# A seventh Strassen block in each channel mixer, and the DRAM weight sums issued during the token mixers

## The chip, the cores and the metric

The kernel runs on one core of one Trainium2 chip, as one launch. The metric is the device time of that launch in microseconds, the median over runs of the same kernel. The profile is of one further execution, taken with the hardware profiler.

## The reference

A two-layer encoder trunk on 512 tokens of width 1024, all in float32. Layer 0 mixes tokens by retention and neighbourhood attention, layer 1 by a bidirectional state-space scan. Each layer then has a channel mixer, and this is what the change is about:

```python
def conv_geglu_ffn(hn, w_up, conv_w, conv_b, w_down):
    u = depthwise_conv_centered(hn @ w_up, conv_w, conv_b)
    gate, val = jnp.split(u, 2, axis=-1)
    return (jax.nn.gelu(gate, approximate=True) * val) @ w_down
```

`hn` is 512 x 1024, `w_up` 1024 x 5632 (2816 gate columns and 2816 value columns), the convolution has width 3 along the tokens, `w_down` is 2816 x 1024. RMS norms stand before and after each mixer, and the result is added to the residual stream.

## The kernel before, in words

**Precision.** Every large product is made of three TensorE passes (`mm3`, L121 to L126): both operands are split into a high part in fp32r and the remainder, and high x high, high x low and low x high are accumulated. ScalarE makes the high part (L115, a cast), VectorE the low part (L116, a subtraction). Each weight tile of 128 x 1024 is split so into one of four places of a ring (`weight`, L81); a place comes free when TensorE has finished with the product four tiles earlier.

**The up projection** (`ffn`). The 2816 hidden columns are 22 tiles of 128, each with a gate and a value half. A plain tile takes two weight tiles of 128 x 1024 and 2 x 8 x 3 matmuls of 512 columns. Pairs of tiles can instead go through one Strassen-Winograd block (`up_strassen`), which forms the 2 x 2 block product of (gate, value) pair weights and (token half, channel half) inputs from seven products in place of eight. Each of the seven is 24 matmuls of 256 columns, 168 in a block. `UP` (L395) lists the first tiles of the blocks: 6, 8, 10 and 14, 16, 18, so two runs of three blocks with the plain tiles 12 and 13 between them; tiles 0 to 5, 20 and 21 are plain too. The combinations of the inputs are made once (`combos`) during tiles 2 to 5.

The seven products of a block (called first to seventh here) need these weight tiles, each split by ScalarE and VectorE: the first q11; the second q12, to which VectorE has added q22 (L458); the third the sum q0 = q11 + q12, made by VectorE; the fourth q0 + q21, added in place by VectorE; the fifth q11 again, to which a DMA issued by GpSimd has by then added another block of `w_up` (L473, an accumulating DMA into SBUF; it overwrites q11, so it waits until the first product's split and VectorE's sum q0 have read it); the sixth q21; the seventh q22. VectorE also does three additions of products (512 columns) in a block, and the tails: per tile four convolution steps (L519, L520) and one multiplication (L527). The tails of a block's two tiles are held back and called during the next block, after its fourth and sixth product, or at once when no block follows.

**The down projection** (`down_strassen`) uses Strassen too. Its combined weights are formed in DRAM: `sums` (L273) makes a list of 32 GpSimd DMAs of 704 KB for each layer ("sums" below), first 16 plain copies of quarters of `w_down`, then 16 accumulating ones. `E.chore()` (L68) issues the next of them and makes it wait for the latest matmul of `E.product`, which only `mm3` sets. Before the change they are issued from: the first pass of the output projection of layer 0's mixer (4), `c` in the last list of `SLOTS` in layer 1's mixer (4), the plain tiles, and `up_strassen` after the second, fourth and sixth product. One preparatory step of the down projection, a subtraction over half of the hidden activations (L320, 128 x 2816 elements, VectorE), needs only tiles 0 to 10.

**What sets the order.** A scheduler orders each engine's instructions when the program is built, by its own estimates; weight splits and loads run ahead of their products. Each engine then works through its list in order and waits where an operand is missing. Weight loads are issued by SyncE (L77, L450) into three `wst` buffers, two `gain` buffers and two `wu` buffers. `PAIRS` and `SLOTS` list the steps of the token mixers in the order in which they are written.

## Time and profile before

| what | value |
|---|---|
| median of 3 runs (lowest, highest) | 1366.14 us (1362.77, 1366.8) |
| the profiled execution | 1365.16 us, of which the span on the core is 1363.4 us |
| TensorE, VectorE, ScalarE, GpSimd busy | 98%, 81%, 61%, 9% of the span |
| DMA, mean over the span | 173 GB/s |
| layer 0: first run of three blocks | 340.88 to 398.47 us |
| layer 0: tiles 12 and 13 | 398.47 to 420.25 us |
| layer 0: second run of three blocks | 420.25 to 482.08 us |
| layer 1: the same three | 1088.34, 1145.93, 1167.72 to 1229.80 us |

The starts are those of the first matmul of each part. A matmul's row ends later than the next one starts, since matmuls are pipelined; what a part costs on TensorE is therefore the distance from its first start to the next part's first start. In the rows, `L126 PE` and so on name the line of the kernel and the engine, `out<-in` the tiles written and read, and `<-DVE ring L116` after an idle time the instruction that ended the wait. PE is TensorE, DVE VectorE, ACT ScalarE, POOL GpSimd, SP SyncE.

### The profile page before, as it was taken

The page shows a single profiled execution, that of the slowest core. Times are in us where ns is not written, and L with a number is a line of the kernel's source. Part 1 is how long each engine was busy: PE and PEld are TensorE (multiplying, and loading weights), DVE is VectorE, ACT ScalarE, POOL GpSimd, SP SyncE. Part 2 cuts the span into 40 slices and gives each one's busy share as a digit, 9 for nine tenths or more (in the row PEclk, how much of TensorE's full clock was granted, in tenths as well). Part 3 has the DMA queues.
Part 4 walks back from the last instruction along what each step waited for, and adds up shares of the span by engine and source line. Part 5 has one row for each costly group of instructions (what it writes and reads, how often), then busy time and mean ns, then how long its engine had stood idle before and what let it go on. Part 6 is the DMA issues. An engine that isn't in the chain of part 4 may idle for free.

```text
span 1363.4 us, 20143 instructions
## 1 busy us (share of the span) xinstructions
PE 1329.6 (98%) x7640; PEld 1135.2 (83%) x7640; DVE 1108.5 (81%) x1536; ACT 831.9 (61%) x1337; POOL 127.6 (9%) x142
## 2 busy tenths in 40 slices
PE   7999999999999999999999999999999999999997
PEld 6877777898998987888778788787879899898886
DVE  7368878696898889797878876898789789899876
ACT  5356667453674666564878787477555466466663
POOL 1011110100111100020000110011011011110001
PEclk9999999999999999999999999999999999999999
DMA  8443234246698966564565455175545678897654
GB/s 299 141 143 102 87 101 156 72 154 206 221 224 189 234 195 203 183 208 129 142 186 190 120 183 171 52 200 151 182 131 193 191 226 211 190 235 197 202 183 147
DMA packets 78785, 236.23 MB, mean 173 GB/s; under 512 B 8544, under 2 KB 9312, under 8 KB 78176
## 3 DMA queue, kind: packets, MB, share of 16 engines
q1 hardware_dynamic: 60368, 167.30, 38.1%
q0 software_dynamic: 10432, 52.43, 16.6%
q10 hardware_dynamic: 7888, 15.21, 4.0%
q8 instruction: 60, 0.98, 0.3%
q14 instruction: 37, 0.30, 0.1%
HBM read 227.30 MB, written 51.64 MB: 205 GB/s over the span
## 4 chain that ended last, share of the span: by engine, by line
PE 74%; DVE 10%; DMA 8%; ACT 4%; issue 3%; POOL 0%; SPq 0%; DVEq 0%; POOLq 0%; ACTq 0%
PE mm L124 20%; PE mm L126 20%; PE mm L125 19%; DMA wst<-in_f_up 3%; DVE ring L116 2%; PE pu L125 2%; DMA pb<-pd 2%; PE pu L126 2%; PE pu L124 2%; PE pi L1133 1%; PE st L1082 1%; ACT ring L115 1%; PE py L1153 1%; DMA wst<-in_c_fm 1%; ACT pb L1112 1%
## 5 line engine op out<-in xcount | busy, mean ns | idle before, releaser
L124 PE MATMUL mm<-xh,ring 128*128 128x512 f32 (+2 forms) x928 | 341.4, 368 | 1.4 <-ACT z L1052 1.0
L126 PE MATMUL mm<-xl,ring 128*128 128x512 f32 (+2 forms) x928 | 340.6, 368 | 1.1 <-DVE mean L936 0.6
L125 PE MATMUL mm<-xh,ring 128*128 128x512 f32 (+2 forms) x928 | 340.2, 367 | 1.0 <-DVE ring L116 1.0
L116 DVE TENSOR_TENSOR ring<-wst,ring 128x1024 fp32r<-128x1024 f32 (+1 forms) x220 | 267.2, 1221 | 61.5 <-ACT ring L115 61.3
L115 ACT CAST ring<-wst 128x1024 fp32r<-128x1024 f32 (+1 forms) x220 | 226.6, 1036 | 133.5 <-PE mm L125 54.0
L124 PEld LDWEIGHTS mm<-xh,ring 128*128 128x128 f32 (+1 forms) x928 | 174.4, 188 | 31.5 <-issue 2.3
L126 PEld LDWEIGHTS mm<-xl,ring 128*128 128x128 f32 (+1 forms) x928 | 174.0, 188 | 30.8 <-issue 1.3
L125 PEld LDWEIGHTS mm<-xh,ring 128*128 128x128 f32 (+1 forms) x928 | 174.4, 188 | 29.3 <-DVE ring L116 1.4
L1112 ACT ACTIVATE pb<-pb,tok 128x128 f32<-128x128 f32 x256 | 81.0, 397 | 10.4 <-DMA pb<-pd 9.3
L124 PE MATMUL mm<-xc,ring 128*128 128x256 f32 x288 | 79.9, 277 | 0.4 <-ACT G L500 0.4
L126 PE MATMUL mm<-xc,ring 128*128 128x256 f32 x288 | 79.8, 277 | 0.0
L125 PE MATMUL mm<-xc,ring 128*128 128x256 f32 x288 | 79.7, 277 | 0.0
L124 PE MATMUL mm<-ring,big 128*128 128x512 f32 x164 | 64.0, 390 | 0.0
L126 PE MATMUL mm<-ring,big 128*128 128x512 f32 x164 | 63.8, 389 | 0.0
L125 PE MATMUL mm<-ring,big 128*128 128x512 f32 x164 | 63.8, 389 | 0.0
L284 POOL DMA_DIRECT2D ts<-in_f_down x48 | 30.6, 638 | 308.2 <-PE mm L126 197.9
L125 PE MATMUL pu<-xh,ring 128*128 128x256 f32 x192 | 54.2, 282 | 4.2 <-DVE ring L116 4.2
L518 ACT ACTIVATE cv<-mm,cwt 128x512 f32<-128x512 f32 x40 | 31.0, 776 | 42.5 <-PE mm L126 42.5
L124 PEld LDWEIGHTS mm<-xc,ring 128*128 128x128 f32 x288 | 54.0, 188 | 0.6 <-ACT G L500 0.6
L126 PEld LDWEIGHTS mm<-xc,ring 128*128 128x128 f32 x288 | 54.1, 188 | 0.0
L125 PEld LDWEIGHTS mm<-xc,ring 128*128 128x128 f32 x288 | 54.0, 188 | 0.0
L126 PE MATMUL pu<-xl,ring 128*128 128x256 f32 x192 | 53.8, 280 | 0.0
(360 smaller groups left out, 3068.8 us busy)
## 6 DMA issues: line engine op xcount, KB each, us to landing
ts<-in_f_down POOLq DMA_DIRECT2D x48, 704.0 KB, 7.1
wst<-in_f_up SPq DMA_DIRECT2D x64, 512.0 KB
wst<-in_c_fm SPq DMA_DIRECT2D x40, 512.0 KB
wst<-ts SPq DMA_DIRECT2D x32, 512.0 KB
pb<-pd ACTq DMA_DIRECT2D x29, 512.0 KB
wst<-in_f_down SPq DMA_DIRECT2D x24, 512.0 KB
ts<-ts POOLq DMA_DIRECT2D x16, 704.0 KB, 9.2
wst<-in_ab_fm SPq DMA_DIRECT2D x20, 512.0 KB
```

What stands on the lines that cost most here:

```text
L115: first = self.nc.scalar.copy(hi, src)
L116: second = self.nc.vector.tensor_tensor(lo, src, hi.bitcast(F32), op=ALU.subtract)
L124: mm(out, lh, rh, start=first, stop=False)
L125: mm(out, ll, rh, start=False, stop=False)
L126: self.product = mm(out, lh, rl, start=False, stop=last)
L284: out.append(lambda i=i, src=src, j=j, c=c, kw=kw: gp.dma_start(part(ts, i, c), part(src, j, c), **kw))
L518: nc.scalar.activation(o, ps, AF.Identity, scale=w(1), bias=w(3))
L1082: nc.tensor.matmul(ps, o["bt"][:, c], xs, start=True, stop=True)
L1112: nc.scalar.activation(pb[:, dr, c], pb[:, dr, c], AF.Identity, scale=1.0 - 2 * dr, bias=tok[:, 0, c, dr * H + h:dr * H + h + 1])
L1133: nc.tensor.matmul(pi[:, c - 1 + dr], o["st"][dr, i][:, q * P:(q + 1) * P], o["t"][1][:, c * C:(c + 1) * C], start=True, stop=True)
L1153: E.together([nc.tensor.matmul(py[j * 64:j * 64 + 64, c * C:(c + 1) * C], o["x"][:, c, (2 * q + j) * 64:(2 * q + j + 1) * 64], ms[j][0][:, c],
```

## The change

Three edits. `UP` gets the entry 12, so tiles 6 to 19 are seven Strassen blocks in a row. `up_strassen` issues a sum after its second and fifth product (before: second, fourth, sixth); the held tails are called where they were. `PAIRS` and three lists of `SLOTS` get steps `c`, each of which issues one sum: 15 in layer 0's mixer, 8 more in layer 1's; and `ret_values` sets `E.product`, so that a sum after it waits for its matmuls.

```diff
-UP = (6, 8, 10, 14, 16, 18)
+UP = (6, 8, 10, 12, 14, 16, 18)
...
-        if i in (1, 3, 5):
+        if i in (1, 4):
             E.chore()
-            if i > 1 and held:
-                held.pop(0)()
+        if i in (3, 5) and held:
+            held.pop(0)()
...
 PAIRS = (
-    "nq rq rk nk rg k d s0 m a0 a1 v0 w0 s2 a2 a3 v2 w1 w2 n w3 o",
+    "nq rq rk nk rg c k d s0 m a0 a1 v0 c w0 s2 a2 a3 v2 c w1 w2 n w3 o",
...
             E.together(ms, [w for _, w in o["sd", i]])
+            E.product = ms[-1]
...
+                elif step == "c":
+                    E.chore()
...
 SLOTS = (
...
-    "s0 G R s1 s2 h0 i0 i1 o0 h1 h2 o1 p0 h4 h3 p1 h5 i2 n0 n1 p2 n6 n3 h6 n7 n2 n9 N i3 n8 h7 p3 n4 n5 N",
+    "s0 G R s1 s2 h0 i0 i1 o0 c h1 h2 o1 c p0 h4 h3 p1 h5 i2 n0 c n1 p2 n6 c n3 h6 n7 n2 n9 N i3 n8 h7 p3 n4 n5 N",
```

What it moves. On TensorE, ScalarE and VectorE the token mixers' instructions stand in the same order as before, and on SyncE too. TensorE loses, in each layer, the 96 matmuls of tiles 12 and 13 and gets one more block of 168.

VectorE, layer 0, where the second run of blocks began before (`gain_3988` is that block's q0, `wst_4167` its follower's q12; the second row is the sum that the fourth product needs, the last its split):

```order
L520 SCALAR_TENSOR_TENSOR cv0_3910<-mm_3856,cwt_2543,cv0_3910 128x511
L458 TENSOR_TENSOR gain_3988<-gain_3988,gain_4018 128x1024
L458 TENSOR_TENSOR wst_4167<-wst_4167,wu_4169 128x1024
L320 TENSOR_TENSOR H_2519<-H_2519 128x11x256
L519 SCALAR_TENSOR_TENSOR cv1_3915<-mm_3885,cwt_2543,cv1_3915 128x511
L116 TENSOR_TENSOR ring_69<-gain_3988,ring_69 128x1024
```

VectorE after the change, from the split for the fifth block's first product (`wst_4009`) to those for its second and third (`wst_4038`, `gain_4070`):

```order
L116 TENSOR_TENSOR ring_69<-wst_4009,ring_69 128x1024
L320 TENSOR_TENSOR H_2534<-H_2534 128x11x256
L458 TENSOR_TENSOR V_3776<-w5_3937,V_3776 128x2x256
L458 TENSOR_TENSOR G_3775<-pu_3779,G_3775 128x2x256
L519 SCALAR_TENSOR_TENSOR cv0_3967<-G_3544,cwt_2558,cv0_3967 128x511
L116 TENSOR_TENSOR ring_69<-wst_4038,ring_69 128x1024
L520 SCALAR_TENSOR_TENSOR cv0_3967<-G_3544,cwt_2558,cv0_3967 128x511
L519 SCALAR_TENSOR_TENSOR cv1_3972<-V_3545,cwt_2558,cv1_3972 128x511
L116 TENSOR_TENSOR ring_69<-gain_4070,ring_69 128x1024
```

The subtraction L320 has moved from just ahead of the split for a fourth product to just behind the split for a first.

ScalarE before, in the third block (`gain_3598` is q0, `wst_3536` is q11 after its accumulating DMA):

```order
L518 ACTIVATE cv1_3664<-V_3300,cwt_2543,cwn_2545 128x512
L115 CAST ring_69<-gain_3598 128x1024
L500 COPY G_3531<-mm_3533 128x2x256
L115 CAST ring_69<-wst_3536 128x1024
L525 ACTIVATE cv0_3659<-cv0_3659 128x512
```

ScalarE after the change, in the sixth block (`gain_4299` is q0, first as the third product's weights and then as the fourth's; `wst_4238` is q11 after its accumulating DMA; `gain_4329` is q21):

```order
L115 CAST ring_69<-gain_4299 128x1024
L500 COPY G_4233<-mm_4235 128x2x256
L115 CAST ring_69<-wst_4238 128x1024
L500 COPY V_4234<-pu_4236 128x2x256
L115 CAST ring_69<-gain_4299 128x1024
L115 CAST ring_69<-gain_4329 128x1024
```

In the first four blocks the cast for the fourth product stands ahead of the one for the fifth; in the fifth, sixth and seventh it stands behind it, in both layers, and so do the splits on VectorE:

```order
L458 TENSOR_TENSOR gain_4299<-wst_4238,wst_4267 128x1024
L519 SCALAR_TENSOR_TENSOR cv0_4359<-G_4004,cwt_2558,cv0_4359 128x511
L527 TENSOR_TENSOR H_2534<-cv0_4196,cv1_4201 128x512
L116 TENSOR_TENSOR ring_69<-gain_4299,ring_69 128x1024
L520 SCALAR_TENSOR_TENSOR cv0_4359<-G_4004,cwt_2558,cv0_4359 128x511
L458 TENSOR_TENSOR gain_4299<-gain_4299,gain_4329 128x1024
L116 TENSOR_TENSOR ring_69<-wst_4238,ring_69 128x1024
L519 SCALAR_TENSOR_TENSOR cv1_4364<-V_4005,cwn_2560,cv1_4364 128x511
L116 TENSOR_TENSOR ring_69<-gain_4299,ring_69 128x1024
```

These nine rows begin with the sixth block's sum q0, after which its accumulating DMA can start, and end with the split for its fourth product.

GpSimd in layer 0's mixer, before and after the change (`rb` is the rotary multiplication of a head pair, `rs` its group norm):

```order
L737 TENSOR_TENSOR rb_679<-rb_679,rot_234 128x512
L737 TENSOR_TENSOR rb_985<-rb_985,rot_234 128x512
L826 TENSOR_TENSOR rs_924<-rs_924,rg_760 128x512
L737 TENSOR_TENSOR rb_1032<-rb_1032,rot_234 128x512
L737 TENSOR_TENSOR rb_1373<-rb_1373,rot_234 128x512
```

```order
L737 TENSOR_TENSOR rb_679<-rb_679,rot_234 128x512
L284 DMA ts0_220<-in_f0_down 16x11264 x3
L737 TENSOR_TENSOR rb_988<-rb_988,rot_234 128x512
L827 TENSOR_TENSOR rs_927<-rs_927,rg_760 128x512
L737 TENSOR_TENSOR rb_1035<-rb_1035,rot_234 128x512
L284 DMA ts0_220<-in_f0_down 16x11264 x4
```

The first head pair's three sums stand ahead of the next pair's first rotary step, the second pair's four ahead of the third pair's, and so on. Of the 32 sums of layer 0, 13 are left to its channel mixer (28 before): 7 in the plain tiles and 2 in each of the first three blocks, none after that. In layer 1 it is 20 (28 before), the last of them in the seventh block.

8 rows, old and new, of tables (PAIRS, SLOTS) are left out of this document.

## The prediction

> **What bounds the kernel now.** I read the page's first lines, then who TensorE waits for, longest first in total (us in total, times, longest).
>
> ```profile
> span 1363.4 us, 20143 instructions
> PE 1329.6 (98%) x7640; PEld 1135.2 (83%) x7640; DVE 1108.5 (81%) x1536; ACT 831.9 (61%) x1337; POOL 127.6 (9%) x142
> PE pt L181 <- DVE xs L172: 10.2, 5, 7.3
> PE pu L125 <- DVE ring L116: 4.2, 2, 2.5
> PE mm L124 <- DVE xf L1046: 1.7, 2, 1.6
> ```
>
> TensorE is the bound. Only the second wait belongs to the blocks: twice, VectorE's split of a block's weights came late. The next view is the busy time of each engine by stretch (length, then per engine busy time and count; clock, DMA share, GB/s). First layer 0: the second and third block of the first run, tiles 12 and 13, the three blocks of the second run, and the sum of these and the first block. Then layer 1: third block, tiles 12 and 13, first block of the second run, the same sum, and 3.41 us out of that block.
>
> ```profile
> 360.07:379.27 19.20, 19.20 (x171) 19.20 (x169) 16.92 (x20) 13.41 (x18) 3.23 (x4) 1.00 0.78 246
> 379.27:398.47 19.20, 19.20 (x171) 19.20 (x169) 18.14 (x23) 14.08 (x19) 2.60 (x3) 1.00 1.01 223
> 398.47:420.25 21.78, 21.78 (x98) 18.02 (x97) 20.61 (x27) 10.96 (x15) 2.12 (x2) 1.00 0.76 190
> 420.25:441.84 21.59, 19.89 (x170) 19.69 (x168) 18.23 (x18) 11.22 (x14) 3.94 (x4) 1.00 0.89 196
> 441.84:461.68 19.84, 19.84 (x171) 19.84 (x169) 15.64 (x18) 12.08 (x17) 3.94 (x4) 1.00 1.05 238
> 461.68:482.08 20.40, 19.99 (x170) 19.79 (x169) 19.57 (x25) 15.10 (x20) 3.52 (x4) 1.00 1.03 244
> sum 141.20, PE 139.09 PEld 134.93 DVE 125.69 ACT 88.07 POOL 22.61; mean PE 19.87 PEld 19.28 DVE 17.96 ACT 12.58 POOL 3.23
> ...
> 1126.73:1145.93 19.20, 19.20 (x170) 19.20 (x169) 17.87 (x23) 13.89 (x19) 2.59 (x3) 1.00 0.99 226
> 1145.93:1167.72 21.79, 21.79 (x98) 18.02 (x97) 19.79 (x26) 10.74 (x14) 2.13 (x2) 1.00 0.73 183
> 1167.72:1191.41 23.69, 21.23 (x170) 21.03 (x169) 19.35 (x19) 11.32 (x14) 3.94 (x4) 0.93 0.89 188
> sum 141.46, PE 139.00 PEld 135.03 DVE 125.52 ACT 88.13 POOL 22.55; mean PE 19.86 PEld 19.29 DVE 17.93 ACT 12.59 POOL 3.22
> 1178.36:1181.77 3.41, 3.00 (x14) 3.00 (x15) 3.41 (x5) 0.00 (x0) 0.00 (x0) 0.50 0.52 94
> ```
>
> A block takes 19.20 us when nothing waits, the two plain tiles 21.78. The second run takes 21.59 + 19.84 + 20.40 = 61.83 us in layer 0 in place of 57.60, so 4.23 are lost there; in layer 1 all seven stretches take 141.46, so 4.47 are lost (141.46 - 115.20 - 21.79). Where, the order of VectorE and TensorE in time shows (start, length, idle time before and what ended it).
>
> ```profile
> 419.89 1.22 DVE L458 TENSOR_TENSOR gain<-gain 128x1024 f32<-128x1024 f32 x1
> 424.47 1.22 DVE L458 TENSOR_TENSOR wst<-wst,wu 128x1024 f32<-128x1024 f32 x1 [3.36 <-DMA wst<-in_f_up]
> 425.61 3.08 DVE L320 TENSOR_TENSOR H<-H 128x2816 f32<-128x2816 f32 x1
> 428.61 0.74 DVE L519 SCALAR_TENSOR_TENSOR cv<-mm,cwt,cv 128x511 f32<-128x511 f32 x1
> 429.27 1.22 DVE L116 TENSOR_TENSOR ring<-gain,ring 128x1024 fp32r<-128x1024 f32 x1
> ...
> 430.54 0.39 PE L125 MATMUL pu<-xh,ring 128*128 128x256 f32 x1 [1.70 <-DVE ring L116]
> 1178.77 0.58 PE L125 MATMUL pu<-xh,ring 128*128 128x256 f32 x1 [2.46 <-DVE ring L116]
> ```
>
> The fourth product's sum was ready at 421, its split ended at 430.5: between them stood an addition for the next block, whose load came 3.36 us late under a DMA share of 0.89, and the subtraction L320. In layer 1 the same wait was 2.46 us, and the clock was at half in the 3.41 us from 1178.36 (0.50, last row above); the block lost 4.49 us (23.69 - 19.20), 2.46 of it in the gap and 0.4 to slower matmuls after it (below), so about 1.5 to the clock.
>
> **The change part by part.** *TensorE.* Each layer exchanges 21.78 us for 19.20: -2.58, certain. The lost 4.23 and 4.47 go too, since the seam after tiles 12 and 13 goes. If VectorE kept up, that would be -13.9 in all. What is late next is VectorE. Its pace when it never waits:
>
> ```profile
> 1158.63 0.74 DVE L520 SCALAR_TENSOR_TENSOR cv<-mm,cwt,cv 128x511 f32<-128x511 f32 x1
> 1159.29 1.21 DVE L116 TENSOR_TENSOR ring<-wst,ring 128x1024 fp32r<-128x1024 f32 x1
> 1160.42 0.74 DVE L519 SCALAR_TENSOR_TENSOR cv<-mm,cwt,cv 128x511 f32<-128x511 f32 x1
> ...
> 1164.00 0.69 DVE L527 TENSOR_TENSOR H<-cv,cv 128x512 f32<-128x512 f32 x1
> 1164.61 1.22 DVE L116 TENSOR_TENSOR ring<-wst,ring 128x1024 fp32r<-128x1024 f32 x1
> ...
> 385.47 1.23 DVE L116 TENSOR_TENSOR ring<-wst,ring 128x1024 fp32r<-128x1024 f32 x1
> 1132.67 1.23 DVE L116 TENSOR_TENSOR ring<-wst,ring 128x1024 fp32r<-128x1024 f32 x1
> ```
>
> From start to start, 1024 columns cost 1.13 us, a convolution step 0.66, 512 columns 0.60, and L320 3.00. A block in the middle of a run has ten of 1024 (seven splits, three sums), eight convolution steps and five of 512: 11.35 + 5.3 + 3.0 = 19.7 us. TensorE needs 19.2. The plain tiles were where VectorE caught up; in a run of seven it falls back 0.5 us a block, and L320 now adds 3.0 in the middle. The count in VectorE's order after the change, from the split for the third block's fifth product (which starts at 385.47 in the trace; nothing before it has moved): up to the sixth block's q0 there are 27 of 1024, 21 steps, 14 of 512 and L320, 56.0 us, so q0 is there at 441.5; up to the split for that block's fourth product it is 63.8 us, 449.3. TensorE, at 19.2 us a block from 340.88, would want that product at 340.88 + 5 x 19.2 + 8.3 = 445.2 (its fourth product starts 8.3 us into a block: 2.88 + 2 x 2.72). So VectorE alone costs 4.1 us.
>
> *The accumulating DMA.* It is worse, since in the sixth block the fifth product's cast and split stand ahead of the fourth's, and the fifth's weights have to land first. The landing of that DMA (L473; the shortest, median and longest from GpSimd's issue), that of a sum (L284), and an example of ScalarE released by the landing:
>
> ```profile
> DMA to landing us min/median/max: 6.0/8.0/10.7
> ...
> DMA to landing us min/median/max: 4.1/7.6/11.4
> ...
> 364.90 1.05 ACT L115 CAST ring<-wst 128x1024 fp32r<-128x1024 f32 x1 [1.15 <-DMA wst<-in_f_up]
> 365.87 0.59 ACT L500 COPY V<-pu 128x512 f32<-128x512 f32 x1
> ```
>
> From q0 to the fourth product: landing, cast 1.05, copy 0.5, cast 1.05, split 1.2. With the shortest landing, 6.0, that is 9.8, so the product starts at 451.3, 6.1 us late in all; with the median, 8.0, it is 8.1. Of this lateness 1.6 falls in the fifth block (the same count up to its fourth product gives 427.6, against 426.0 wanted); the rest, over 4 us, is one gap, longer than the one that brought the half clock: 1.5 us more. I take 6.0 in layer 0, where no sums are issued any more at that point, and 8.0 in layer 1, where two a block still are (VectorE stands 0.3 earlier there: 1132.67 against 385.47 + 747.46). The seventh block repeats the order; with 10 us of work and landing after q0 again it just holds in layer 0 and loses about 1.2 in layer 1. After a wait the matmuls of 256 columns have come 0.1 us a product slower (19.84 against 19.20 for a whole block): 0.4. So layer 0: 7 x 19.2 + 6.1 + 1.5 + 0.4 = 142.4 against 141.2, **+1.2**; layer 1: 134.4 + 7.8 + 1.5 + 1.2 + 0.4 = 145.3 against 141.5, **+3.8**. The ends: VectorE alone, landing never late, no half clock, 134.4 + 4.1 in each, -5.7 in all; both layers at a landing of 10.7, some 5 us beyond layer 0's 6.1 and 3 beyond layer 1's, +13.
>
> The Trainium skill (TensorE: Matmul & The Clock Gate, Part 1: The HAM clock gate) says that the clock halves after an idle window of about 3.4 us that runs freely. The trace shows it after a gap of under 3 us, so the measured row decides; by the page a gap of 4 us is halved as well, and the sum would be the same up to the place of the window.
>
> *The sums.* 15 more run in layer 0's mixer, 8 more in layer 1's. The share of the software queue, two stretches of those mixers by engine, and two loads of layer 1's from the chain of waits:
>
> ```profile
> q0 software_dynamic: 10432, 52.43, 16.6%
> 110.00:200.00 90.00, 89.22 (x519) 71.99 (x518) 72.39 (x143) 58.81 (x105) 10.10 (x7) 1.00 0.28 89
> 740.00:860.00 120.00, 118.25 (x611) 95.88 (x610) 88.15 (x127) 93.36 (x201) 8.71 (x5) 1.00 0.50 154
> 842.67 7.29 DMA pb<-pd
> 891.36 10.90 DMA wst<-in_c_fm
> ```
>
> 16.6% of 1363 us for 52.4 MB is 4.3 us a MB, so a sum of 0.72 MB fills all 16 DMA engines for 3.1 us. With shares of 0.28 and 0.50 there is room, and TensorE has its operands: I take 0. The other end is that each of layer 1's eight sums delays a load like the two shown by 3.1 us, and a third of that reaches TensorE: +8. GpSimd's rotary steps behind a sum cost nothing: the sums wait for matmuls that run before the next pair's rotation, and GpSimd is 9% busy.
>
> A sum adds no wait on another engine; GpSimd alone waits. Fewer sums in the blocks can't gain below the case "VectorE alone", since VectorE's count is the same.
>
> So 1365.2 + 1.2 + 3.8 + 0 = 1370.2 in the frame of the profiled execution. It lies 1.0 us below the median of the three runs, which spread over 4.0; I forecast **1370.5**.
>
> **The rivals.** *VectorE keeps up* (-13.9, 1351): its 23 operations in the third blocks (18.14, 17.87 busy of 19.20) show no wait of TensorE, and three blocks in a row did not fall behind. Against it: 19.7 is more than 19.2, those runs began with VectorE ahead, and L320 has to stand somewhere. Chance 0.08. *VectorE alone* (-5.7, 1359.5): with 23 sums gone from the blocks the accumulating DMA lands early enough that the order of casts costs nothing, and the gap stays short of the half clock. For it: with the 4.1 us in which a sum has landed, 4.1 + 3.8 = 7.9 us from q0 to the fourth product would equal the 7.8 (449.3 - 441.5) of VectorE's own work. Against: the shortest landing of this DMA is 6.0. Chance 0.22. *The mixers pay* (1374 to 1381): loads that are late already (10.9 us for one of 512 KB) are later with sums beside them; it decides as soon as a sum falls together with a load that ScalarE waits for. Chance 0.2. The Trainium skill (Trainium Kernel Development and Optimization, Key Constraints) says that DMAs of all issuing queues share the same 16 engines, which speaks for this rival; the time by it is the 3.1 us a sum worked out above. *It does not do what it says*: excluded for TensorE, whose order shows the exchange.
>
> **How the numbers follow.** A measurement here tells 0.3%, 4.1 us, from no change: faster is below 1362.0, slower above 1370.2. The forecast case (1366 to 1374) has 0.42, 0.24 of it slower and 0.18 the same; "keeps up" 0.08, faster; "VectorE alone" 0.22, 0.14 faster and 0.08 the same; "the mixers pay" 0.2, slower; 0.08 is left for mixtures, which I count as the same 0.05 and slower 0.03. Faster 0.22, same 0.31, slower 0.47. The range leaves out "keeps up" and the far end of the mixers: 1358 to 1379; the forecast's own is 1366 to 1374.
>
> **What would show it.** Right: in each layer's blocks TensorE waits for L116 in the fifth and sixth block, the longest over 3 us in the sixth just behind a cast released by a `wst` landing, with a clock of 0.50 after it; VectorE nearly without idle time from the fourth block on. Wrong: seven stretches of 19.2 (then VectorE keeps up), gaps under 2 us without the half clock (VectorE alone), or mixers that end later than before: layer 0's blocks at 340.9, layer 1's 747.5 us after layer 0's.

## The result, and the profile after

| | before | after |
|---|---|---|
| median of the runs (lowest, highest) | 1365.34 us (1362.77, 1366.8) | 1382.74 us (1379.07, 1385.44) |
| ratio, 95% interval | | 1.0128 (1.0103 to 1.0153) |
| the profiled execution | 1365.16 us | 1385.44 us |

The kernel became slower by 17.4 us, 1.3%; the forecast had been slower by some 5. Its direction held, its time (1370.5) and range (1358 to 1379) didn't. The profiled executions differ by 20.3 us. This is where they lie, from the first starts on TensorE:

| stretch | before | after | difference | forecast |
|---|---|---|---|---|
| up to layer 0's first block | 340.88 | 346.05 | +5.2 | 0 |
| layer 0, first block | 19.2 | 24.6 | +5.4 | 0 |
| layer 0, tiles 8 to 19 | 122.0 | 128.7 | +6.7 | +1.2 |
| layer 0, tiles 20 and 21 and down stage | 130.4 | 128.3 | -2.1 | 0 |
| layer 1, mixer and tiles 0 to 5 | 475.9 | 473.2 | -2.7 | 0 |
| layer 1, tiles 6 to 19 | 141.5 | 149.2 | +7.8 | +3.8 |
| the rest | 126.7 | 126.7 | 0 | 0 |

The last stretch ends with the end of TensorE's last matmul. First the page of the changed kernel, as far as it answers to the lines shown of before.

```profile
span 1383.7 us, 20464 instructions
PE 1337.5 (97%) x7784; PEld 1148.5 (83%) x7784; DVE 1123.2 (81%) x1554; ACT 840.8 (61%) x1353; POOL 132.0 (10%) x144
```

TensorE is still the bound, with 144 more instructions and 7.9 us more busy time. That is no measure of the loss: a waiting engine isn't busy. Whom it waited for (us in total, times, longest):

```profile
PE pt L181 <- DVE xs L172: 10.2, 4, 7.3
PE pu L124 <- ACT ring L115: 9.7, 4, 4.4
PE mm L124 <- ACT G L500: 3.6, 2, 3.1
PE y L874 <- ACT w L866: 2.7, 2, 1.5
```

The first row stands in both profiles. The other three weren't among the longest waits of before, and each is one place of the table: a cast that came late in the sixth blocks, a copy that came late in layer 0's first block, and the attention values in layer 0's mixer. The busy time by stretch shows the first and the third to sixth block of layer 0, the fifth and sixth of layer 1, and the three stretches of the blocks in which the clock was at half (length, busy time of each engine with its count, clock, DMA share, GB/s):

```profile
346.05:370.62 24.57, 21.51 (x169) 21.31 (x168) 18.09 (x19) 11.10 (x14) 3.96 (x4) 0.93 0.70 153
...
389.82:409.02 19.20, 19.20 (x171) 19.20 (x169) 19.16 (x24) 13.29 (x19) 2.99 (x3) 1.00 0.88 211
409.02:429.98 20.96, 19.89 (x171) 19.70 (x169) 19.02 (x20) 13.03 (x17) 1.21 (x1) 1.00 0.60 146
429.98:451.45 21.47, 20.54 (x171) 20.04 (x169) 21.47 (x27) 13.77 (x19) 0.00 (x0) 1.00 0.43 121
451.45:479.47 28.02, 23.15 (x170) 22.36 (x169) 21.67 (x25) 14.19 (x19) 2.42 (x2) 0.88 0.33 77
...
1180.12:1201.58 21.46, 20.53 (x171) 20.03 (x169) 21.46 (x27) 13.87 (x19) 1.83 (x2) 1.00 0.75 186
1201.58:1229.92 28.34, 23.36 (x171) 22.66 (x170) 21.68 (x25) 14.18 (x19) 4.34 (x4) 0.88 0.68 146
...
354.87:358.28 3.41, 3.41 (x16) 3.41 (x17) 3.41 (x4) 2.32 (x3) 0.00 (x0) 0.50 0.93 184
464.09:470.92 6.83, 5.91 (x24) 5.32 (x25) 5.57 (x7) 3.30 (x5) 0.00 (x0) 0.50 0.48 154
1215.02:1221.85 6.83, 6.21 (x27) 5.91 (x28) 4.99 (x7) 2.73 (x5) 0.00 (x0) 0.50 0.50 157
```

In the fifth blocks VectorE has no idle time at all (21.47 of 21.47, 21.46 of 21.46); the sixth blocks are the costliest, 28 us, with half the clock for 6.83 us. The sixth block of layer 0 in time (start, length, what it waited for):

```profile
452.73 1.22 DVE L458 TENSOR_TENSOR gain<-wst 128x1024 f32<-128x1024 f32 x1
...
454.60 1.21 POOL L473 DMA_DIRECT2D wst<-in_f_up  x1 [25.98 <-DVE cv L520]
...
457.58 1.22 DVE L458 TENSOR_TENSOR gain<-gain 128x1024 f32<-128x1024 f32 x1
462.02 1.04 ACT L115 CAST ring<-wst 128x1024 fp32r<-128x1024 f32 x1 [6.51 <-DMA wst<-in_f_up]
462.97 0.58 ACT L500 COPY V<-pu 128x512 f32<-128x512 f32 x1
463.10 1.23 DVE L116 TENSOR_TENSOR ring<-wst,ring 128x1024 fp32r<-128x1024 f32 x1 [4.30 <-ACT ring L115]
463.45 1.99 ACT L115 CAST ring<-gain 128x1024 fp32r<-128x1024 f32 x2
...
464.55 0.58 PE L124 MATMUL pu<-xh,ring 128*128 128x256 f32 x1 [4.41 <-ACT ring L115]
```

The fourth product's sum is made from 457.58 and ready by 459, but ScalarE's cast of it stands behind the fifth product's cast, and that waits until 462.02 for the DMA that was issued at 454.60, 7.4 us. TensorE waits 4.41 us (4.7 from start to start of its matmuls). This is the chain that the prediction described, at the place that it named.

Layer 0's first block waits for something else. Rows of the changed kernel: two DMAs of GpSimd, SyncE's load of weights for the second block's second product, VectorE's addition to them, and what stands behind that addition:

```profile
335.98 1.25 POOL L473 DMA_DIRECT2D wst<-in_f_up  x1 [10.28 <-DVE ring L116]
336.77 1.46 POOL L284 DMA_DIRECT2D ts<-ts  x1
338.88 0.37 SPq L450 DMA_DIRECT2D wst<-in_f_up  x1
...
348.97 1.23 DVE L458 TENSOR_TENSOR wst<-wst,wu 128x1024 f32<-128x1024 f32 x1 [6.59 <-DMA wst<-in_f_up]
...
352.02 1.22 DVE L458 TENSOR_TENSOR gain<-gain 128x1024 f32<-128x1024 f32 x1
353.28 1.05 ACT L115 CAST ring<-gain 128x1024 fp32r<-128x1024 f32 x1 [1.03 <-DVE gain L458]
354.23 0.58 ACT L500 COPY G<-mm 128x512 f32<-128x512 f32 x1
354.87 0.58 PE L124 MATMUL mm<-xc,ring 128*128 128x256 f32 x1 [3.06 <-ACT G L500]
```

The load took 10.1 us (338.88 to 348.97); in the same place of a run that left the sums where they were (the first experiment) it took 5.5. The addition that waits for it belongs to the next block, but in VectorE's list it stands ahead of the sum for this block's fourth product (352.02); in ScalarE's list the cast of that sum (353.28) stands ahead of the copy of the first product (354.23), and for that copy TensorE waits 3.06 us before its third product. The prediction showed the same step as a cause in the kernel before (its row at 424.47, an addition for the next block that waits 3.36 us for a load), but didn't look for it here.

Before the load, six sums had been issued in tiles 0 to 5, as in the kernel before, but with 15 sums done in the mixer these six were accumulating ones; they landed in 9.5 us at the median, 12.7 at the longest (7.0 and 8.3 us for the six copies of that other run). The one in the second row landed after 11.7 us, 0.5 us ahead of the load.

In layer 0's mixer, the rows around a sum issued behind the retention values of the first pair (step `v2`, L812; the expectations call them attention values):

```profile
104.71 0.49 POOL L284 DMA_DIRECT2D ts<-in_f_down  x1 [8.38 <-PE y L812]
...
109.47 0.69 DVE L738 TENSOR_TENSOR ra<-ra,rot 128x512 f32<-128x512 f32 x1 [0.97 <-DMA rb<-ra]
109.51 1.78 POOL L737 TENSOR_TENSOR rb<-rb,rot 128x512 f32<-128x512 f32 x1 [4.32 <-ACT sq L820]
110.08 1.62 DVE L856 TENSOR_SCALAR e<-e,sm 128x256 f32<-128x256 f32 x2
...
114.94 1.09 PE L874 MATMUL y<-w,nvt 128*64 128x128 f32 x14 [1.28 <-ACT w L866]
```

The small DMA `rb<-ra` that turns the halves for the next pair's rotation arrives later than in the kernel before, where GpSimd's step on it starts at 104.46 (2.3 of the 5.0 us are older, see the last section); now that step falls on VectorE's L856 (1.62 for two that take 0.6 alone), and TensorE waits at the end of that chain.

### The profile page after: what moved, and what is told of

Its sections match the earlier page's. It is cut to its first block, busy times and chain, and to the rows that moved or that the text cites. A ratio compares the mean times of both kernels' runs of the same rounds, so it can differ in the third digit from the quotient of the medians.

```text
span 1383.7 us, 20464 instructions
## 1 busy us (share of the span) xinstructions
PE 1337.5 (97%) x7784; PEld 1148.5 (83%) x7784; DVE 1123.2 (81%) x1554; ACT 840.8 (61%) x1353; POOL 132.0 (10%) x144
## 4 chain that ended last, share of the span: by engine, by line
PE 51%; DVE 7%; ACT 5%; DMA 5%; issue 2%; POOL 0%; DVEq 0%; POOLq 0%; ACTq 0%
PE mm L124 13%; PE mm L126 13%; PE mm L125 13%; DMA wst<-in_f_up 2%; DMA pb<-pd 2%; DVE ring L116 2%; PE pu L125 2%; PE pu L126 2%; PE pu L124 2%; ACT pb L1115 1%; PE pi L1136 1%; PE st L1085 1%; ACT ring L115 1%; PE py L1156 1%; PE pd L126 1%
## 5 line engine op out<-in xcount | busy, mean ns | idle before, releaser
L116 DVE TENSOR_TENSOR ring<-wst,ring 128x1024 fp32r<-128x1024 f32 (+1 forms) x218 | 263.4, 1214 | 77.9 <-ACT ring L115 77.4
L124 PE MATMUL mm<-xh,ring 128*128 128x512 f32 (+1 forms) x880 | 321.4, 366 | 1.2 <-DVE xf L1049 0.6
L126 PE MATMUL mm<-xl,ring 128*128 128x512 f32 (+2 forms) x880 | 320.5, 365 | 1.1 <-DVE mean L939 0.6
L125 PE MATMUL mm<-xh,ring 128*128 128x512 f32 (+2 forms) x880 | 320.2, 364 | 1.1 <-DVE ring L116 1.1
L115 ACT CAST ring<-wst 128x1024 fp32r<-128x1024 f32 (+1 forms) x218 | 224.1, 1033 | 141.3 <-PE mm L125 62.7
L124 PEld LDWEIGHTS mm<-xh,ring 128*128 128x128 f32 x880 | 165.6, 188 | 28.8 <-issue 3.0
L126 PEld LDWEIGHTS mm<-xl,ring 128*128 128x128 f32 (+1 forms) x880 | 165.1, 188 | 28.3 <-issue 1.3
L125 PEld LDWEIGHTS mm<-xh,ring 128*128 128x128 f32 (+1 forms) x880 | 165.6, 188 | 27.0 <-DVE ring L116 1.5
L124 PE MATMUL mm<-xc,ring 128*128 128x256 f32 x336 | 94.7, 282 | 3.6 <-ACT G L500 3.6
L125 PE MATMUL mm<-xc,ring 128*128 128x256 f32 x336 | 94.3, 281 | 0.0
L126 PE MATMUL mm<-xc,ring 128*128 128x256 f32 x336 | 94.2, 280 | 0.0
L1115 ACT ACTIVATE pb<-pb,tok 128x128 f32<-128x128 f32 x256 | 80.7, 392 | 12.0 <-DMA pb<-pd 10.9
L124 PE MATMUL pu<-xh,ring 128*128 128x256 f32 x224 | 65.7, 293 | 10.9 <-ACT ring L115 9.7
L124 PEld LDWEIGHTS mm<-xc,ring 128*128 128x128 f32 x336 | 64.0, 191 | 4.1 <-ACT G L500 4.0
L125 PE MATMUL pu<-xh,ring 128*128 128x256 f32 x224 | 65.1, 291 | 2.3 <-DVE ring L116 2.2
L126 PE MATMUL pu<-xl,ring 128*128 128x256 f32 x224 | 64.4, 287 | 0.0
L124 PE MATMUL mm<-ring,big 128*128 128x512 f32 x164 | 64.0, 390 | 0.0
L125 PEld LDWEIGHTS mm<-xc,ring 128*128 128x128 f32 x336 | 63.9, 190 | 0.0
L126 PEld LDWEIGHTS mm<-xc,ring 128*128 128x128 f32 x336 | 63.9, 190 | 0.0
```

What stands on the lines that cost most here:

```text
L115: first = self.nc.scalar.copy(hi, src)
L116: second = self.nc.vector.tensor_tensor(lo, src, hi.bitcast(F32), op=ALU.subtract)
L124: mm(out, lh, rh, start=first, stop=False)
L125: mm(out, ll, rh, start=False, stop=False)
L126: self.product = mm(out, lh, rl, start=False, stop=last)
L1115: nc.scalar.activation(pb[:, dr, c], pb[:, dr, c], AF.Identity, scale=1.0 - 2 * dr, bias=tok[:, 0, c, dr * H + h:dr * H + h + 1])
```

## The experiments

Theory A, formed from these rows: the sums cost 3 us in the mixer (their place), 5 in the first block (their kind, accumulating), and in the blocks the loss is the landing with the order of casts on top of VectorE's backlog. The rivals are in the expectations: that the run of seven costs it all (B), that VectorE alone makes the gap (E), that sums beside the accumulating DMA make it (C). All runs in one table; the third column is the time between the first matmuls of the retention states (L781 in the kernel before) for the first and for the fourth pair, which holds the three sums in question and nothing of the start:

| kernel | ratio to before (interval) | pairs 1 to 4 | layer 0, first block | layer 0, tiles 8 to 19 | layer 1, tiles 6 to 19 |
|---|---|---|---|---|---|
| before | | 125.8 | 19.2 | 122.0 | 141.5 |
| after | 1.0128 (1.0103, 1.0153) | 128.6 | 24.6 | 128.7 | 149.2 |
| seven_only | 1.0078 (1.0057, 1.0100) | 125.8 | 19.2 | 129.5 | 148.5 |
| sums_only | 0.9979 (0.9960, 0.9997) | 128.6 | 23.7 | 119.2 | 139.6 |
| order | 1.0076 (1.0049, 1.0102) | 129.3 | 22.8 | 124.4 | 147.4 |
| late | 1.0002 (0.9987, 1.0018) | 128.8 | 23.9 | 119.1 | 140.3 |
| late_no_v2 | 0.9996 (0.9980, 1.0012) | 125.9 | 26.0 | 119.2 | 140.6 |
| late_no_tile | 1.0007 (0.9989, 1.0025) | 128.6 | 19.2 | 123.2 | 140.6 |
| late_quiet0 | 1.0113 (1.0075, 1.0152) | 125.9 | 19.2 | 132.6 | 145.7 |
| late_both | 0.9960 (0.9938, 0.9982) | 125.8 | 19.2 | 121.9 | 140.3 |
| no_block_sums | 1.0069 (1.0045, 1.0093) | 128.9 | 22.0 | 125.2 | 145.8 |
| late_both2 | 0.9971 (0.9955, 0.9987) | 125.9 | 19.2 | 122.0 | 141.0 |
| three_both | 0.9947 (0.9928, 0.9967) | 125.8 | 19.2 | 119.2 | 139.2 |
| three_both_late | 0.9937 (0.9918, 0.9957) | 125.9 | 19.2 | 118.7 | 140.2 |
| late_less | 0.9923 (0.9897, 0.9948) | 125.9 | 19.2 | 121.6 | 137.0 |
| late_pool | 0.9988 (0.9961, 1.0015) | 125.8 | 19.2 | 121.9 | 142.5 |

**The two halves alone.** `seven_only` is the kernel before with only the first edit, `sums_only` the changed kernel with the old list of blocks.

```diff
-UP = (6, 8, 10, 14, 16, 18)
+UP = (6, 8, 10, 12, 14, 16, 18)
```

> Half of the change: seven blocks in a row, but the sums where they were before (three in each block, none added in the mixers). Theory A (read from the two traces): the change lost 20 us in four places: 5 in layer 0's mixer, 5 in the first block of layer 0, where accumulating sums slow a load, 7 to 8 a layer in the fifth and sixth blocks against what the exchange of products gives, and got back 2.4 in layer 1's mixer and 2.5 in layer 0's down stage. By it, without the moved sums: layer 0's blocks begin at 340.9 us as before, its first block takes 19.2 us, the sixth still has a gap of over 4 us, each layer's seven blocks take 148 to 150 us, and the time is 1373 to 1378. Theory B: the run of seven alone costs it all and the place of the sums is free: 1382. Theory C: the sums beside the accumulating DMA in each block make its landing later, as it was in the kernel before (median 8.0 us): the sixth block's gap grows to 6 us or more, and the time is 1380 or above, with the loss inside the blocks.

Measured 1377.68 us. The mixer and the first block (19.20 us) are as before, and both layers' blocks about as long as in the change, layer 0's sixth with a gap of 5.5 us:

```profile
442.78:471.88 29.10, 23.45 (x171) 22.66 (x170) 21.70 (x25) 14.18 (x19) 4.60 (x5) 0.82 0.74 158
```

A's time range holds, at its upper end. B is wrong: the run of seven alone costs 11 us, not 17. The gap and the time of C (6 us, 1380) aren't reached.

> The other half: two runs of three with tiles 12 and 13 plain as before, the sums moved as in the change. Theory A: layer 0's blocks begin 3 to 5 us later than before (346), its first block has the gap of about 3 us and the half clock after it (24 us in place of 19.2), layer 1's mixer ends 2 us earlier, and the late fourth product of the fifth tile pair is about as before: 1368 to 1373. Theory B (the place of the sums is free): 1365, within 2 us, with layer 0's blocks beginning at 341 to 343. Theory D: fewer sums beside the accumulating DMA bring the fourth product in time, and the 8 us lost in the second runs go: 1357 to 1361.

Measured 1363.18 us, a little faster than before, and so under A's range. Mixer (128.6) and first block cost what A says:

```profile
343.95:367.67 23.72, 21.41 (x169) 21.21 (x168) 18.09 (x19) 11.09 (x14) 3.96 (x4) 0.93 0.76 161
427.85:447.82 19.97, 19.88 (x169) 19.68 (x168) 17.37 (x17) 10.78 (x13) 1.21 (x1) 1.00 0.41 114
1170.07:1190.39 20.32, 19.88 (x169) 19.68 (x168) 17.36 (x17) 10.77 (x13) 4.09 (x4) 1.00 0.82 182
```

But what D says is there as well: the late fourth product of the second runs goes (19.97 and 20.32 in place of 21.59 and 23.69 us), so the sums outside the blocks pay for their own cost. D's time (1357 to 1361) isn't reached, since the mixer and the first block cost. The bad half of the change is the seventh block. The halves don't add up to the 17 us of the change (11 more, 4 less): in the run of seven those late fourth products aren't there to be won back, while the mixer and the first block cost the same.

**The order of the casts.**

```diff
-        E.split(hi, lo, st)
+        with tc.issue_after(q['cast'].ins) if i == 4 else nullcontext(): q['cast'] = E.split(hi, lo, st)
```

> The changed kernel with one thing forced: the cast and split for a block's fifth product (whose weights come from the accumulating DMA) are issued behind those for its fourth, in every block. VectorE's work and all DMAs stay. Theory A (the landing and the order of casts make the gap of 4.6 to 4.7 us in the sixth block): that gap falls to under 2.5 us, the half clock behind it goes or is one window, and the two layers' blocks are 3 to 5 us shorter each: 1373 to 1377. Theory E (VectorE's backlog alone makes it): the gap stays above 3.5 us and the time at 1381 to 1384.

Measured 1375.16 us. The sixth blocks:

```profile
450.35:473.29 22.94, 20.79 (x170) 20.08 (x169) 21.88 (x25) 14.17 (x20) 2.42 (x2) 1.00 0.40 96
1193.41:1219.98 26.57, 23.53 (x170) 22.74 (x169) 21.88 (x25) 14.16 (x20) 4.34 (x4) 0.87 0.61 130
```

In layer 0 the gap of 4.7 us falls into three of 0.8 to 1.2 us (from start to start, as all gaps from here on), none of which brings the half clock, and the block is 5.1 us shorter. In layer 1 it is only 1.8: the gap ahead of the fourth product falls to 1.0 us, but the fifth product now waits 2.06 us, and the clock halves behind that. The time and the gap ahead of the fourth product are A's; that each layer's blocks fall by 3 to 5 us isn't: it is 6.1 in layer 0 and 1.8 in layer 1. E is wrong: VectorE's lateness alone, with the order put right, makes no gap above 2.1 us in the sixth blocks. The run changes a little more than the order of two casts: behind the forced order a few other steps of the last blocks moved too (on VectorE some convolution steps and the addition for the next block). What is left of the sixth blocks (22.9 and 26.6 us against 19.2) I put down to that lateness, in smaller pieces, and the clock.

**The subtraction out of the run.**

```diff
-            tt(A21, A11, A21, op=ALU.subtract)
+            with tc.issue_after(E.seventh.ins): tt(A21, A11, A21, op=ALU.subtract)
...
-            add(o, r, o)
+            E.seventh = add(o, r, o)
```

> The changed kernel with one thing forced: the 3.0 us subtraction for the down stage (L320) is issued behind the seventh block, among tiles 20 and 21, in place of in the fourth. In the order that comes out, the cast for the fifth product also stands behind that for the fourth in blocks 5 to 7. Theory A (backlog 3.0 too long plus the order): no gap over 1 us in blocks 2 to 7 of either layer, each layer's blocks within 1 us of 134.4 but for layer 0's first block, which keeps its gap of 3 us and its half clock: 139 and 135, so 1383 - 14 - 14 = 1355; with 2 us given back in the down stage, 1357. Theory F (VectorE falls back 0.5 us a block whatever is moved, and a gap comes in the last blocks all the same): gaps of 1 to 3 us in blocks 6 and 7, 1365 to 1375.

Measured 1367.62 us: between A and F, in F's range. No gap over 1.9 us is left in blocks 2 to 7, and the sixth blocks take 19.84 and 20.92 us:

```profile
449.40:469.24 19.84, 19.84 (x171) 19.84 (x169) 19.80 (x24) 13.71 (x19) 1.21 (x1) 1.00 0.42 109
1188.75:1209.67 20.92, 20.26 (x170) 19.86 (x169) 19.83 (x24) 13.66 (x19) 3.08 (x3) 1.00 0.85 193
```

Beyond the order, taking L320's 3.0 us away is worth 5.3 us in layer 0's tiles 8 to 19 (124.4 to 119.1) and 7.1 us in layer 1 (147.4 to 140.3). The last four blocks still take 1.0 us more than 19.2 each in layer 0 and 1.5 in layer 1, on average, so VectorE falls back as F says; but the longest gaps stand in the fourth blocks (1.8 and 1.0 us), not in the sixth and seventh.

**No sums in the blocks.**

```diff
-            E.chore()
+            E.chore(0)
...
-        assert not E.chores
+        E.chores.clear()
```

> The changed kernel without the two sums a block (the others stay): it leaves the last sums out, 4 in layer 0 and 11 in layer 1. The orders of casts and splits stay as in the change but for the sums. Theory A (the accumulating DMA lands late because sums are beside it, and the order of casts turns that into the gap): its landings fall to 4 to 6 us, the sixth block's gap to under 3 us in both layers, blocks 2 to 7 take 120 to 124 us in layer 0 (128.7 in the change) and layer 1's seven 139 to 143 (149.2): 1368 to 1374. Theory E (VectorE's backlog alone): the gap in the sixth block stays at 4 us or above, and both layers stay within 2 us of the change. Layer 0's first block keeps its gap by both.

Measured 1374.56 us, just above A's range. 15 sums are left out, and on the other four engines every instruction stands where it stood. The landings fell to a median of 6.1 us (A: 4 to 6), but the gaps stayed, 4.42 and 5.48 us, as E says; the blocks became 3.5 us a layer shorter, less than A says and more than E:

```profile
444.67:471.89 27.22, 22.61 (x171) 21.82 (x170) 21.67 (x25) 14.16 (x19) 2.39 (x2) 0.87 0.33 80
1191.94:1219.85 27.91, 22.24 (x170) 21.45 (x169) 21.68 (x25) 14.19 (x19) 2.42 (x2) 0.88 0.30 77
```

So A is wrong on the cause of a long landing in the sixth block: there it is 7.1 and 8.2 us without any sum beside it, and by the prediction's sum a landing of 6 us would be enough for the gap as long as the order of casts stands. That E alone isn't the cause rests on `order`, where VectorE's work is the same and the gap goes. What the sums in the blocks do cost is elsewhere: without them the third and fourth blocks take 19.2 us in both layers (the fourth 20.96 and 20.94 with them). In layer 0's fourth a landing of 10.9 us had held up a cast, and behind it in ScalarE's order a copy that TensorE waits for (1.1 us). It is 3.5 us a layer in all.

**Where the sums stand.** Five kernels on top of `late`. Without the three sums behind the attention values:

```diff
-    "nq rq rk nk rg c k d s0 m a0 a1 v0 c w0 s2 a2 a3 v2 c w1 w2 n w3 o",
+    "nq rq rk nk rg c k d s0 m a0 a1 v0 c w0 s2 a2 a3 v2 w1 w2 n w3 o",
...
```

(and the same in the lines of the second and third pair)

> The kernel with L320 late, and in layer 0's mixer three sums less: those that are issued behind the attention values of the first three pairs, just ahead of the next pair's rotation. All other sums stay (each comes one to three places earlier in the chain, so that more are copied and fewer accumulated before the blocks). Theory A (these three sums stand beside the small DMA that turns the halves for the rotation, and that alone made layer 0's mixer 3.0 us longer): the two gaps of 1.5 to 2.0 us at the transposed attention values (about 113 and 196 us) go, and layer 0's blocks begin at 340.9 to 341.5, or up to 3.8 us later if the start or the collision of VectorE and GpSimd at 80 us falls badly, which is seen ahead of 90 us; the time is 3 us shorter, 1364 to 1365. Theory G (any sums in that mixer cost, 0.2 us each): the gaps get smaller but stay, and 0.6 us are won. The first block keeps its gap (22.5 to 24 us) by both.

Measured 1365.04 us. The mixer is back at 125.9 us and layer 0's blocks begin at 340.78. The rotation's rows are those of before, though the sums ahead of it in the pair still run:

```profile
104.39 1.33 POOL L737 TENSOR_TENSOR rb<-rb,rot 128x512 f32<-128x512 f32 x1 [10.54 <-DMA rb<-ra]
...
106.67 0.66 DVE L738 TENSOR_TENSOR ra<-ra,rot 128x512 f32<-128x512 f32 x1
```

A is right on the mixer, G wrong: three sums cost 2.9 us, the other 12 in that mixer nothing that the trace shows. The first block is still long, 26.0 us, longer than the 22.5 to 24 expected, though layer 0's blocks begin where they did before the change. Without the sums in tiles 0 to 5, and (`late_both`) without both:

```diff
             tail(f, *p0[f])
-            E.chore()
+            E.chore(0)
...
-            E.chore(1 + (f == 2))
+            E.chore(int(f > UP[0]))
```

> The kernel with L320 late, and without the sums issued in tiles 0 to 5 (seven a layer): they are then issued in the blocks' own places, two a block, and in tiles 20 and 21. Theory A (accumulating sums in tiles 0 to 5 hold up the load of the first block's second product in layer 0): layer 0's first block takes 19.2 to 19.6 us in place of 23.9, and the time is 4 to 5 us shorter, 1363. Theory H (the block's own two accumulating sums, or the first accumulating DMA of the block, hold up that load): the first block still takes 22 us or more and the time stays at 1367. What could come back by either: the last sums end later, and the down stage of layer 0 waits for them as in the kernel before, 2 us.

> The kernel with L320 late and both cuts: no sum behind the attention values of the first three pairs, none in tiles 0 to 5. Theory A: 3 and 4.5 us are won and at most 2 given back in the down stage: 1359 to 1362, the fastest of these four with a seventh block, layer 0's blocks in 138 to 139 us. Theory G and H: 1366 or above.

Measured 1366.72 and 1361.57 us; both leave the last four sums of layer 1 out, as too few places were left for them there. Layer 0's first block takes 19.2 us in both, so A is right on it and H wrong. The 138 to 139 us that A gives for `late_both`'s blocks in layer 0 are missed, it is 141.1.

The time of the first fell by only 0.9 us of the 4.7 won: the sums that now run beside the later blocks cost 4.1 us there (123.2 against 119.1). The down stage, where I had expected 2 us to be given back, is as long as before the cut (128.3 us). With the tiles' sums left in layer 1 and all sums made, `late_both2`:

> Seven blocks, L320 late, no sum behind the attention values of the first three pairs; in layer 0 alone none in tiles 0 to 5; all sums are made. In layer 1 the sums are those of the change. Layer 0 as in the kernel with both cuts (blocks from 341.0, 141.1 us long), layer 1 as with L320 late alone (140 to 141 us): 1360 to 1363. If L320 in tiles 20 and 21 costs nothing and VectorE then sets the last four blocks, these take 20.2 to 21.5 us each in both layers.

Measured 1362.15 us, as expected. Three sums in each block, and in layer 0 none in the pairs of the mixer:

```diff
-        if i in (1, 4):
+        if i in (1, 3, 4):
             E.chore()
...
```

> The kernel with L320 late; in layer 0 the sums are where they were in the kernel before (none in the mixer's pairs, three in a block), in layer 1 a third sum in each block is allowed but none is left for the last ones, as 12 are in the mixer. Theory A: layer 0's blocks begin at 340.9 to 342.5, the first block takes 19.2 us, and though the accumulating DMA lands later beside three sums a block, the order of casts behind the late subtraction leaves it room, so the seven blocks take 138 to 140 us; the down stage of layer 0 gets its 2 us back: 1367 - 3 - 4.5 + 2 = 1361 to 1362. Theory C (sums beside the accumulating DMA delay it whatever the order): gaps of over 2 us in blocks 4 to 6, 142 us or more, 1365 or above.

Measured 1381.39 us. Mixer and first block as A says, but the blocks as C says, 24.3, 26.3 and 23.8 us for the fourth to sixth of layer 0. The rows are layer 0's fourth and layer 1's fifth; behind the latter, with the sums used up, layer 1's sixth takes 19.19 us:

```profile
398.56:422.84 24.28, 20.27 (x170) 19.87 (x169) 20.79 (x24) 14.51 (x20) 3.90 (x4) 1.00 0.93 213
...
1179.94:1203.38 23.44, 21.64 (x171) 21.44 (x169) 19.84 (x24) 13.78 (x19) 3.42 (x3) 0.93 0.82 187
```

The accumulating DMA lands in 8.8 us at the median here (7.5 in `late`).

**What sets the last blocks.** On top of `late_both2`, first with VectorE's second convolution step left out of the blocks' tiles, then with the addition behind the fifth product on GpSimd.

```diff
-            nc.vector.scalar_tensor_tensor(o[:, :S - 1], ps[:, 1:], w(2), o[:, :S - 1], op0=ALU.mult, op1=ALU.add)
+            less or nc.vector.scalar_tensor_tensor(o[:, :S - 1], ps[:, 1:], w(2), o[:, :S - 1], op0=ALU.mult, op1=ALU.add)
...
-            add(V[:, :, low], t, V[:, :, low])
+            nc.gpsimd.tensor_tensor(V[:, :, low], t, V[:, :, low], op=ALU.add)
```

> The kernel with seven blocks, L320 late and the sums moved out of the two bad places, without the second of the two convolution steps on VectorE in the tiles that Strassen blocks make (L520): it leaves a third of their convolution out, 4 steps or 2.6 us of VectorE a block. If VectorE's pace sets the last four blocks (20.2 to 21.1 us each), all seven blocks of both layers fall to 19.2, within 0.3, 134.4 to 136 us a layer, and the time falls by 12 us to 1350. If the accumulating DMA and the casts behind it set them, they stay above 20 us and the time falls by less than 4.

Measured 1357.11 us: 5 to 7 us less (by the medians, by the ratios), between the two. In layer 1 the last four blocks fall to 19.2, so there VectorE set them; a new wait of the second block costs 2 there and 2.4 in layer 0. In layer 0 the fifth and sixth stay at 20.9 and 20.2, where VectorE itself waits, up to 4.58 us, for a load of weights. Its rows, fifth block of layer 1 and of layer 0:

```profile
1165.12:1184.32 19.20, 19.20 (x171) 19.20 (x169) 16.60 (x20) 13.70 (x18) 3.15 (x3) 1.00 0.89 202
420.72:441.60 20.88, 19.79 (x170) 19.59 (x169) 16.30 (x19) 13.37 (x18) 3.13 (x3) 1.00 0.80 181
```

> The same kernel with nothing left out, but the addition behind each block's fifth product (0.60 us of VectorE a block) made by GpSimd. If VectorE's pace sets the last four blocks and GpSimd doesn't slow it, each is 0.6 us shorter, 5 us in all: 1357. If GpSimd and VectorE slow each other while both read and write the on-chip memory (in layer 0's mixer a step of 0.69 us took 1.83 us beside one of GpSimd), or if the accumulating DMA behind it in GpSimd's order is issued later, the time stays or rises: 1361 to 1368.

Measured 1366.66 us, no gain. Of its rows, the two that run beside each other:

```profile
1162.06 2.64 POOL L498 TENSOR_TENSOR V<-w,V 128x512 f32<-128x512 f32 x1
...
1163.45 1.79 DVE L519 SCALAR_TENSOR_TENSOR cv<-G,cwt,cv 128x511 f32<-128x511 f32 x1
1164.65 1.26 POOL L473 DMA_DIRECT2D wst<-in_f_up  x1
```

The 0.6 us taken from VectorE come back as 1.0 on its next step (1.79 in place of 0.75), and the accumulating DMA is issued only behind GpSimd's 2.64 us.

**The best of both.** The six blocks of before with the sums in the mixers, none of them in the two bad places, without and with L320 late:

> The place of the sums without the seventh block, mended: two runs of three, the sums in the mixers, but none behind the attention values of the first three pairs and none in layer 0's tiles 0 to 5. From the run with the sums moved alone (1363.2), less 3.0 in the mixer, less 4.5 in the first block, and 2 to 4 given back in layer 0's down stage, whose sums end later: 1357 to 1360. If the late fourth product comes back in layer 0's second run, where more sums stand now, 1361 to 1364.

> The same with L320 issued behind the last block. If VectorE has room in the plain tiles 12 and 13 as they are, L320 costs and gains nothing in the second run: the same time as without, within 2 us. If the late splits of the second run came from L320, up to 2 us a layer are won: 1354 to 1358.

Measured 1358.28 and 1356.58 us, 0.53% and 0.63% faster than before and 1.8% to 1.9% faster than the change. Whether L320 gains there is inside the spread. It has the same cuts as `late_both2` (1362.15 us) but six blocks in place of seven, so with all three repairs the seventh block doesn't pay: the 2.6 us a layer that it saves TensorE are given back, in layer 1 as VectorE sets the pace (`late_less`), in layer 0 for a part that stays open.

## Why the prediction failed, step by step

- **TensorE's exchange, -2.58 a layer.** It is in the trace: the third block of layer 0 takes 19.20 us, and no plain tiles stand in the run. The losses of 4.2 and 4.5 us behind the plain tiles I had put down to that seam and to L320. `sums_only` keeps both, and there layer 0's tiles 8 to 19 lose 1.4 us against 117.8 without a wait, layer 1's tiles 6 to 19 2.6 against 137.0; so 2.8 of the 4.2 us in layer 0 and 1.9 of the 4.5 in layer 1 went with the moved sums, without a seventh block.
- **VectorE's count.** Right. From the split for the third block's fifth product to the end of the sixth block's q0 it was 56.0 us of work; the changed kernel takes 58.1 (395.76 to 453.86) with one wait of 1.94 in it, so 56.2. That L320 matters in the run: `late`.
- **The order of casts and the landing.** Right in place, chain and size of the gap: over 4 us forecast in the sixth block, 4.4 and 4.3 waited (L124 for L115). It rests on `order`, and on `late`, where the order comes out right as well. What I took for the difference of the layers (6.0 us of landing without sums, 8.0 with) was wrong: 7.4 and 7.3 in the sixth blocks, and without sums no better.
- **The half clock, 1.5 us a layer: mis-sized.** 6.83 us at half are 3.4 us lost, in each layer, since the row of before that I took it from had 3.41 us. That is +1.9 twice. The last section shows when a second piece follows.
- **The blocks ahead of the sixth: mis-sized.** I had 1.6 us in the fifth and 0.4 for slower matmuls behind waits. The fourth and fifth blocks lost 1.8 and 2.3 in layer 0, the third to fifth 0.7, 1.7 and 2.3 in layer 1. Part of it is a chain that I had not seen: in layer 0's fourth block a landing of 10.9 us holds a cast, and ScalarE's copy behind it holds TensorE. Without sums in the blocks the third and fourth take 19.2 us, so it is the sums' doing; the fifth still take 21.2 there, so that is not. In layer 1 I didn't find one wait that carries it, a product merely takes 2.83 us for 2.72 through whole blocks.
- **"The sums ... I take 0": the step that failed.** It cost 2.9 us in layer 0's mixer and 5.4 in layer 0's first block. I looked at the mean DMA share of the mixers (0.28 and 0.50) and at what waits for large loads, not at the 64 KB DMA that stands next to a sum, and in the sentence on GpSimd's rotary steps I asked when GpSimd is free, not when their data arrive. And I counted the sums that leave the blocks, not which ones take the places in tiles 0 to 5: the copies there became accumulating DMAs, and beside them the load for the second block took 10.1 us in place of 5.5. What is shown is that the block takes 19.2 us without sums in those tiles (`late_no_tile`) or with copies there (`seven_only`, `late_quiet0`). That the kind alone does it isn't: in layer 1 the sums issued last before the first block are accumulating ones too, and it takes 19.2 us. There the sum ahead of the load comes 2.2 us behind the block's accumulating DMA (1088.36, 1090.58) and lands in 7.9 us; in layer 0 it comes 0.8 us behind (335.98, 336.77) and lands in 11.7. No run parts the two. The rival "the mixers pay" had the right kind of price (3.1 us) but layer 1 for its place, where a cost of the 12 sums doesn't stand out of the spread (next point).
- **Parts that no step foresaw, and that I don't lay to the sums.** Layer 0's mixer was 2.3 us later by the first matmul of the retention states, through a collision at 79.8 us, ahead of the first sum (86.3), and a half clock behind it (last section); in seven other kernels with that sum, without the collision and without a late start, that matmul comes at 89.5 to 89.8 us, against 89.6 before. Layer 1's mixer and tiles 0 to 5 took 473.2 us against 475.9; over all these kernels that stretch lies between 472.3 and 477.5 us, 473.1 in `seven_only`, which leaves that mixer as it was, so a single profile tells nothing here. The down stage of layer 0 took 2.1 us less, as in all kernels but `seven_only` (0.4 less); there TensorE had waited 1.4 us for splits (L116), 1.1 in `seven_only` and not at all in the changed kernel. Which of the edits does it wasn't followed further.

Sum: 5.0 forecast, +2.9 and +5.4 for the sums, +5.5 and +4.0 in the blocks, +2.3, -2.7 and -2.1 for the last point, 20.3.

## What to carry to other kernels

When work is moved to where resources are idle on average, look at which small transfer stands beside each new place, and at what takes the places that it left: here three of 15 moved DMAs cost 3 us, and places that kept their number of DMAs but got accumulating ones for copies cost 5 in one layer and nothing in the other. Where one engine works through a list in order, put nothing that waits for a DMA ahead of what the bound engine wants sooner. A longer run of the denser form pays only as long as the second-busiest engine keeps up: here it needed 19.7 us a block by the prediction's count where TensorE needed 19.2, and each recovery stretch that is taken out has to be paid for.

## What the runs showed of the hardware

**VectorE and GpSimd block each other, by who starts first.** Two steps of layer 0's first rotation, in the kernel before and in the changed one:

```profile
79.74 0.69 DVE L739 TENSOR_TENSOR ra<-ra,rb 128x512 f32<-128x512 f32 x1
79.75 1.83 POOL L737 TENSOR_TENSOR rb<-rb,rot 128x512 f32<-128x512 f32 x1 [0.67 <-DMA rb<-ra]
```

```profile
79.78 1.29 POOL L737 TENSOR_TENSOR rb<-rb,rot 128x512 f32<-128x512 f32 x1 [0.65 <-DMA rb<-ra]
79.78 1.83 DVE L739 TENSOR_TENSOR ra<-ra,rb 128x512 f32<-128x512 f32 x1
```

The two steps start within 15 ns of each other, and which of them takes 1.83 us differs between executions, with no difference in the program up to there. With GpSimd first TensorE came 2.3 us later to the next step, a half clock of 3.41 us in it (0.9 us in `order` and `late_pool`, where the same happened without a half clock). The Trainium skill (SBUF — State Buffer, SBUF: two separate sides) says that a VectorE operation with two on-chip inputs and a GpSimd operation exclude each other for the whole instruction, and that the first to start has it; these rows agree.

**The half clock comes in pieces of 3.41 us, and the length of a gap alone doesn't tell how many.** Gaps from start to start of 2.73 us (before, layer 1) and 3.33 us (the first block) brought one such piece, 4.4 to 5.4 us two, 5.46 us in `seven_only` three (0.82 of 29.10 us), but 5.48 us in `no_block_sums` two. One of 1.99 us in `late_less` brought none, one of 2.06 in `order` (behind two of 1.0 and 0.8 us) and one of 2.07 in `late_quiet0` did; but 3.08 us (`order`, layer 0's first block) and 3.11 us (`late_quiet0`, layer 0's fourth) brought none.

What tells it is where the gap lies. In each trace all changes of the clock stand whole multiples of 3.413 us apart, to 0.01 us (after the first one, at 10 to 17 us), and so mark off windows, differently in each execution. Counted between 30 and 1345 us in all 16 traces, the 17 windows at full clock in which no matmul's row runs for 1.80 us or more were all followed by half clock, and of the others one was (1.63 us, in the changed kernel's mixer). At half clock, full clock came back behind each window with at most 0.41 us without a matmul, and behind none with 0.47 or more. The gap of 3.11 us is cut by an edge into 1.50 and 1.33 us, the one of 2.07 lies in one window with 1.80. So whether a gap of 2 to 3.5 us is punished is partly luck; one of over 3.6 us, as in the sixth blocks, holds more than 1.8 us in one of two windows wherever it lies (an estimate from these figures).

The Trainium skill (TensorE: Matmul & The Clock Gate, Part 1: The HAM clock gate) gives a free-running window of about 3.4 us. With that the pieces and the multiples agree; that it takes a window without work doesn't, since windows with 1.6 us of work in 3.4 were enough.
